# The first two modulation vectors of layer 0 from slabs of columns, and two of the other four as dots on VectorE

## The chip, the cores and the metric

The kernel runs on one NeuronCore of a Trainium2 chip. The metric is the device time of one launch in microseconds. The core has a matrix engine (TensorE, PE in the profile, with PEld for its weight loads), VectorE (DVE), ScalarE (ACT) and GpSimd (POOL), each with its own queue of instructions that it takes in order, and a sync engine (SP) that issues nearly all loads from memory, also in order. An instruction that has to wait for a semaphore holds up everything behind it in its queue.

## The reference

Two layers work on 512 tokens `x` and on 256 context tokens `ctx`, both 1024 wide. Each layer draws six vectors from a condition, `c` for the tokens and `c_ctx` for the context: shift, scale and gate for the mixer (vectors 0, 1, 2), and shift, scale and gate for the FFN (3, 4, 5).

```python
mod  = silu(c)     @ ada_w[l] + ada_b[l]          # 1024 x 6144, six vectors of 1024
modc = silu(c_ctx) @ ada_w[l] + ada_b[l]
sh1, sc1, g1, sh2, sc2, g2 = split(mod, 6)
a  = rmsnorm(h,  norm1_g[l]) * (1 + sc1)  + sh1   # ac from hc with the context's vectors
...
u, v, q, k, vv = split(a @ w_in, ...)             # layer 0: v gated MLP, differential attention
q, k = rope(q), rope(k)                           # layer 1: sliding window attention with a sink
...
h = h + g1 * y
h = h + g2 * swiglu(rmsnorm(h, norm2_g[l]) * (1 + sc2) + sh2)
```

In layer 0 the keys and values of the context stand behind those of the tokens. The mixer needs vectors 0 and 1 of layer 0 before its first product; vectors 2 to 5 are wanted only after its attention.

## The kernel before

Everything is kept transposed: the 1024 features lie on the partitions as 8 tiles (`KT`), tokens along the free axis, 512 columns for `x` (`TX`) and 256 for the context (`TC`). Every large product runs as three fp32r matmuls, high by high, high by low and low by high parts (`mm3`, L96 to L102). A weight block comes through `unit` (L67): SP loads the raw block, ScalarE casts the high part (L75), and GpSimd subtracts to get the low part (L78). The rings behind it have 5 raw buffers and 6 finished ones, and layer 0's q/k weights have three buffers more (`wq`).

The code is written in the order in which the work is meant to go, and a scheduler that simulates a timeline turns it into one queue for each engine; `issue_after` holds an instruction behind another, and a buffer that is allotted again brings a wait for its last reader.

The stage that the change touches is the first part of `even()`, up to the gated products:

- *Start.* `x` is loaded in four pieces, then `ident`. ScalarE takes Silu of `c` and `c_ctx` into `cst`, a tile with 32 columns for each k of which two are not zero. `squares` (L185) and `rstd_diag` (L139, sums on TensorE at L150) give the norm of the tokens, and `spread` (L177) puts it on all partitions.
- *Vectors 1 and 0.* `ada_load` (L339) loads 1 MB pieces of 256 rows by 1024 columns into a ring of four buffers, `ar`. `ada_step` (L347) multiplies one 128-row part by `cst`: four matmuls with 32 rows of output each (L351); in fp32 each stands twice in the profile. `ada_out` (L354) copies the sum, transposes it and adds the bias, and so writes columns of `mod`. First all of vector 1 (scale) is summed, then L394 multiplies the eight tiles of `x` by scale and norm, then all of vector 0 (shift). Between the steps stand filler matmuls without a use of their own (`warm`, L373; L376 issues them).
- *q and k in two halves* (L441). Each half makes four outputs of 128 rows from 8 tiles; for tile k it loads one 256 KB q/k block. In half 0 the shift is added on the way (L457 on ScalarE for the high part, L458 on VectorE for the low part). The context is loaded after the slabs, its norm formed inside half 0, and its eight tiles modulated by `modulate` (L190): VectorE multiplies (L193), ScalarE adds the shift and rounds (L194), VectorE subtracts for the low part (L195). After the token products of a half come those with the context, and `rope` (L242): a shuffle and a product on VectorE (L245, L246), a product and a sum on GpSimd (L247, L248).
- *Vectors 2 to 5* are done as 16 more steps (2 and 3 together, then 4 and 5), strewn through the halves and the following v products (L492) by `ada_ahead`, which loads, and `ada_some`, which computes. These steps have 1 MB each and the same four buffers.
- *v products*, then the attention of the first heads and the gated products (accumulated in `pf`).

Layer 1 has another way to form such vectors, which the changed kernel uses too. `ada_c` (L204) loads `c` spread over all partitions and takes its Silu; `ada_dot` (L219) multiplies a tile of transposed weights by it on VectorE and adds along the row (L222):

```python
self.nc.vector.scalar_tensor_tensor(junk, t, 1.0, self.cb[who], ALU.mult, ALU.mult,
                                    accum_out=self.acc[who][:, col:col + 1])
```

`ada_fin` (L225) adds the bias. One such dot gives 128 values of one vector for one of the two conditions.

Of the kernel before, what the change touches and what calls it, by code (L numbers as in the profile page):

```python
# [14 lines left out]
P = 128  # L15
# [11 lines left out]
class Builder:  # L27
# [286 lines left out]
    def even(self):  # L314
        tc, nc, a = self.tc, self.nc, self.a
        self.open_ring(512, 5, 6)
        self.adap = tc.alloc_tile_pool(name="ada0", bufs=1, side="left", reuse_waits="tile")
        self.ropep = tc.alloc_tile_pool(name="rope0", bufs=1, side="left", reuse_waits="tile")
# [13 lines left out]
        self.ident = self.load(p0, a["ident"], [P, P], "ident")  # L332
# [6 lines left out]
        def ada_load(j, n, k):  # L339

            m = 2 // n
            t = self.adap.tile([P, m, n * D], F32, name=self.uid("ar"), tag="ar", bufs=4)
            src = a["ada0"][k * P:(k + m) * P, j * D:(j + n) * D].rearrange("(k p) c -> p k c", p=P)
            self.last_slab = nc.sync.dma_start(t, src)
            return [t[:, i, :] for i in range(m)]
# [8 lines left out]
        def ada_out(j, n, ps, pt):  # L354
# [8 lines left out]
            for who in range(2):  # L363
                nc.vector.tensor_tensor(q(self.mod[who]), v[:, :, :, who], q(self.adab), ALU.add)
                for i in range(j, j + n):
                    if i in (1, 4):
                        m = self.mod[who][:, i * KT:(i + 1) * KT]
                        nc.vector.scalar_tensor_tensor(m, m, 1.0, self.gain(i // 3, 0), ALU.add, ALU.mult)
            return row
# [9 lines left out]
        slabs = sum([ada_load(1, 1, k) for k in range(0, KT, 2)], [])  # L379
        self.adab = self.load(p0, a["ada_b"], [P, 96], "adab")  # L380
        self.gains = self.load(p0, a["gains"], [P, 5 * KT], "gains")
        rd = self.rstd_diag([(sq, TX)], 1.0 / D)[0]
        ps0 = self.fill()
        for k in range(KT):
            ada_step(ps0, k, slabs[k])
            if k % 2:
                slabs += ada_load(0, 1, k - 1)
            if k == 3:
                rx = self.spread(rd)
            warm(slabs[k][:, :P], 2)  # L390
        scaled = self.bank()
        ada_out(1, 1, ps0, scaled)
        for k in range(KT):
            nc.vector.scalar_tensor_tensor(hx[k], hx[k], self.modcol(0, 1, k, 0), rx, ALU.mult, ALU.mult)  # L394
        ps0 = self.fill()
        for k in range(KT):
# [17 lines left out]
        def ada_some():  # L414
            if loaded:
                j, k, t = loaded.pop(0)
                if k == 0:
                    ps_of[j] = self.fill()
# [985 lines left out]
```

## Time and profile before

| | |
|---|---|
| time, median of 3 runs | 1640.96 us (1637.72 to 1641.31) |
| profiled execution, from its first to its last instruction | 1641.9 us, mean granted clock 0.977 |
| TensorE busy | 1542.8 us (94%) |
| VectorE, ScalarE, GpSimd busy | 1073.0 (65%), 724.5 (44%), 766.9 us (47%) |
| moved by DMA | 161.98 MB, mean 99 GB/s |
| chain of waits | 69% on TensorE |

The profile is of one further execution; for it only the span from its first to its last instruction is known, and the runs give whole device times. A row of the trace gives the time from the start of the span, the duration, the engine, the line, the operation, the buffer written and the buffers read, and in brackets the idle time before it and what ended it. A group row gives a count and the busy time. The table of stretches has, for each engine, the busy time and the number of instructions, and behind that the granted clock of TensorE, the share of the 16 DMA engines that was busy, and the rate.

### The profile page before, as it was taken

Reading aid. Unit: us, or ns where it says so; the run is one execution under the profiler, and the core shown is the slowest. Engines: PE = TensorE matmul, PEld = TensorE weight load, DVE = VectorE, ACT = ScalarE, POOL = GpSimd, SP = SyncE. Lnnn points to the kernel's source line nnn. Section 1 sums busy time; section 2 is a strip of 40 time slices with the busy share of each in tenths; the row PEclk is TensorE's granted clock in tenths of the full one; section 3 lists DMA queues with packets and bytes.
Section 4 is the critical chain, followed back from the end, with each engine's and each line's share of the span. In section 5 each row is a group of like instructions: output and inputs, shape, how many; then the busy total and the mean of one; then the engine's idle time right before and its main releaser. Section 6 shows DMA issues by size and latency. Waiting matters only on the chain.

```text
span 1641.9 us, 24642 instructions
## 1 busy us (share of the span) xinstructions
PE 1542.8 (94%) x9547; PEld 1367.1 (83%) x9547; DVE 1073.0 (65%) x1980; ACT 724.5 (44%) x1472; POOL 766.9 (47%) x543
## 2 busy tenths in 40 slices
PE   6999989999999999999999988999989999999996
PEld 4776877899899889998989978777868989898886
DVE  4621788756857788666665585665667857666665
ACT  2423675645533233333333244555664544444443
POOL 0463221062157666666666316532222466675662
PEclk9999989999999999999999999999999999999998
DMA  8744100141223343343432012110233222322201
GB/s 317 298 153 169 40 7 1 65 139 68 76 79 116 105 139 131 105 150 126 142 131 77 27 51 91 52 33 25 74 116 123 65 103 92 101 90 103 90 27 52
DMA packets 47957, 161.98 MB, mean 99 GB/s; under 512 B 5472, under 2 KB 9952, under 8 KB 40160
## 3 DMA queue, kind: packets, MB, share of 16 engines
q1 hardware_dynamic: 47696, 160.28, 28.4%
q8 instruction: 75, 1.23, 0.3%
q14 instruction: 42, 0.34, 0.1%
q10 hardware_dynamic: 144, 0.13, 0.0%
HBM read 158.29 MB, written 2.10 MB: 98 GB/s over the span
## 4 chain that ended last, share of the span: by engine, by line
PE 69%; DVE 11%; POOL 6%; DMA 5%; ACT 4%; issue 3%; POOLq 0%; SPq 0%; DVEq 0%; ACTq 0%
PE pw L100 9%; PE pw L101 9%; PE pw L102 9%; PE pb L100 7%; PE pb L101 7%; PE pb L102 7%; POOL w L917 5%; DMA raw<-ffn_in 3%; PE pf L100 3%; PE pf L101 2%; PE pf L102 2%; PE pb L1257 2%; PE pb L1246 2%; PE pf L351 2%; DVE t L968 2%
## 5 line engine op out<-in xcount | busy, mean ns | idle before, releaser
L100 PE MATMUL pw<-ax,w 128*128 128x384 f32 (+2 forms) x732 | 237.5, 328 | 16.1 <-DVE q L1012 6.7
L101 PE MATMUL pw<-ax,w 128*128 128x384 f32 (+2 forms) x732 | 237.9, 325 | 4.1 <-DVE ax L458 2.5
L78 POOL TENSOR_TENSOR w<-raw,w 128x512 fp32r<-128x512 f32 (+1 forms) x84 | 127.6, 1526 | 243.2 <-ACT w L75 220.8
L102 PE MATMUL pw<-ax,w 128*128 128x384 f32 (+2 forms) x732 | 236.7, 325 | 2.1 <-POOL w L917 2.1
L917 POOL TENSOR_TENSOR w<-raw,w 128x512 fp32r<-128x512 f32 x119 | 177.7, 1507 | 54.2 <-ACT w L913 53.4
L917 POOL TENSOR_TENSOR w<-t,w 128x512 fp32r<-128x512 f32 x90 | 133.4, 1482 | 139.9 <-ACT w L913 136.5
L100 PE MATMUL pb<-hh,w 128*128 128x512 f32 x480 | 167.3, 362 | 12.8 <-ACT hh L116 8.3
L766 DVE SCALAR_TENSOR_TENSOR xT<-pb,mod,xT 128x512 f32<-128x512 f32 (+3 forms) x208 | 144.5, 704 | 43.8 <-PE pb L102 43.1
L101 PE MATMUL pb<-hh,w 128*128 128x512 f32 x480 | 171.2, 358 | 0.5 <-POOL hh L117 0.5
L102 PE MATMUL pb<-hh,w 128*128 128x512 f32 x480 | 170.7, 357 | 0.0
L100 PEld LDWEIGHTS pw<-ax,w 128*128 128x128 f32 x732 | 142.0, 195 | 27.2 <-DVE q L1012 8.1
L100 PE MATMUL pw<-T,w 128*128 128x384 f32 (+1 forms) x508 | 159.1, 314 | 4.8 <-DVE hs L1008 2.4
L101 PE MATMUL pw<-T,w 128*128 128x384 f32 (+1 forms) x508 | 158.6, 312 | 4.0 <-DVE T L117 4.0
L102 PE MATMUL pw<-T,w 128*128 128x384 f32 (+1 forms) x508 | 158.2, 312 | 0.0
L101 PEld LDWEIGHTS pw<-ax,w 128*128 128x128 f32 x732 | 142.6, 195 | 12.1 <-DVE ax L458 3.4
L102 PEld LDWEIGHTS pw<-ax,w 128*128 128x128 f32 x732 | 142.4, 195 | 6.0 <-POOL w L917 2.7
L913 ACT CAST w<-t 128x512 fp32r<-128x512 f32 x104 | 64.5, 621 | 176.8 <-DVE t L968 122.5
L917 POOL TENSOR_TENSOR w<-rawo,w 128x512 fp32r<-128x512 f32 x63 | 94.1, 1493 | 66.5 <-ACT w L913 66.5
L100 PEld LDWEIGHTS pb<-hh,w 128*128 128x128 f32 x480 | 89.5, 189 | 27.0 <-ACT hh L116 10.8
L100 PEld LDWEIGHTS pw<-T,w 128*128 128x128 f32 x508 | 97.2, 192 | 9.7 <-DVE hs L1008 3.9
L101 PEld LDWEIGHTS pw<-T,w 128*128 128x128 f32 x508 | 97.4, 192 | 6.6 <-DVE T L117 4.6
L102 PEld LDWEIGHTS pb<-hh,w 128*128 128x128 f32 x480 | 90.3, 188 | 13.1
(363 smaller groups left out, 4056.7 us busy)
## 6 DMA issues: line engine op xcount, KB each, us to landing
raw<-ffn_in SPq DMA_DIRECT2D x44, 1024.0 KB, 4.9
ar<-ada SPq DMA_DIRECT2D x24, 1024.0 KB, 7.3
ar<-ada SPq DMA_DIRECT2D x48, 512.0 KB, 3.5
rawo<-ffn_out SPq DMA_DIRECT2D x44, 512.0 KB, 3.9
raw<-odd_out SPq DMA_DIRECT2D x32, 256.0 KB, 2.7
raw<-qk SPq DMA_DIRECT2D x16, 256.0 KB, 7.9
raw<-uv SPq DMA_DIRECT2D x16, 256.0 KB, 2.7
raw<-even_out SPq DMA_DIRECT2D x8, 512.0 KB, 4.2
```

The costliest lines, as they stand in the source:

```text
L78: eng.tensor_tensor(lo, raw, hi.bitcast(F32), ALU.subtract)
L100: mm(out, s[0], m[0], start=start, stop=False, **kw)
L101: mm(out, s[0], m[1], start=False, stop=False, **kw)
L102: return mm(out, s[1], m[0], start=False, stop=stop, **kw)
L351: nc.tensor.matmul(ps[32 * q:32 * q + 32, :w], cst[:, k, :], t[:, w * q:w * q + w], start=k == 0, stop=k == KT - 1, skip_group_check=True)
L766: self.nc.vector.scalar_tensor_tensor(h, ps[:, r], self.modcol(l, j, m, who), h, ALU.mult, ALU.add)
L913: nc.scalar.copy(t[:, 0, :], src)
L917: eng.tensor_tensor(t[:, 1, :], src, t[:, 0, :].bitcast(F32), ALU.subtract)
L968: nc.vector.tensor_tensor(t, x, y, how)
L1246: last = nc.tensor.transpose(pt[:, x * P:(x + 1) * P], es[2 * (x % 2) + x // 2][:, kb * P:(kb + 1) * P], self.ident)
L1257: nc.tensor.matmul(po[64 * h:64 * h + 64, :], V[vb][:, 64 * g:64 * g + 64], t[:, h * TC:h * TC + TC], start=kb == 0, stop=kb == nb - 1, sk ...
```

## The change

The weights of vectors 0 and 1 are laid out anew on the host: slab k holds, in 1 MB without gaps, the columns of both vectors that tile k needs, for all eight row tiles (`ada_s`). So tile k of `x` can be modulated when slab k alone has been projected. `first_rows` multiplies a slab by `cst`, four row tiles side by side in the four quarters of the partitions, and `first_cols` adds the four partial sums and transposes them in one step, with two small matmuls by `sel`; the results go into `first`. The tiles of `x` are multiplied by the norm first, then scaled and shifted by one VectorE instruction, then split. The products of tile k - 2 follow the projection of slab k. The fillers are now six behind each of the first three slabs, and those behind vectors 1 and 0 go.

Vectors 2 and 3 are transposed on the host (`ada_t`) and done as dots on VectorE: eight tiles of 1 MB, four dots each, strewn through the same places by `ada_some`. Vectors 4 and 5 stay steps on TensorE, and come behind them. The ring `ar` has three buffers in place of four, and the pool also holds the two spread conditions (`cb`). `ident`, the bias and the gains go to ScalarE's queue for loads; the context is loaded behind slab 3, and the spread conditions and the rope tables behind the last q/k block of half 0. The context is modulated between the products of tiles 6 and 7 and reads `first`. Line numbers in the diff's `first_rows` and after are those of the changed kernel: `slab` is L351, `first_rows` L355 to L364, `first_cols` L366 to L375, the product with the norm L486, scale and shift L493.

```diff
-        self.ident = self.load(p0, a["ident"], [P, P], "ident")
+        self.ident = self.load(p0, a["ident"], [P, P], "ident", eng=nc.scalar)
+        self.adab = self.load(p0, a["ada_b"], [P, 96], "adab", eng=nc.scalar)
+        self.gains = self.load(p0, a["gains"], [P, 5 * KT], "gains", eng=nc.scalar)
 
...
-        def ada_load(j, n, k):
-
-            m = 2 // n
-            t = self.adap.tile([P, m, n * D], F32, name=self.uid("ar"), tag="ar", bufs=4)
-            src = a["ada0"][k * P:(k + m) * P, j * D:(j + n) * D].rearrange("(k p) c -> p k c", p=P)
-            self.last_slab = nc.sync.dma_start(t, src)
-            return [t[:, i, :] for i in range(m)]
+
+        sel = self.adap.tile([P, 2], F32, name="sel")
+        nc.vector.tensor_reduce(sel, self.ident.rearrange("p (q c) -> p c q", q=4)[:, 0:2, :], axis=AX, op=ALU.add)
+        one_b = self.adap.tile([P, KT], F32, name="one_b")
+        nc.vector.tensor_scalar(one_b, self.adab[:, KT:2 * KT], 1.0, None, ALU.add)
+        first = self.adap.tile([P, 2, KT, 2], F32, name="first")
+
+        def slab(k):
+            t = self.adap.tile([P, 2 * D], F32, name=self.uid("ar"), tag="ar", bufs=3)
+            self.last_slab = nc.sync.dma_start(t, a["ada_s"][k])
+            return t
+
+        def first_rows(t):
+
+            ps = self.fill()
+            for r in range(2):
+                for q in range(4):
+                    k = 4 * r + q
+                    nc.tensor.matmul(ps[32 * q:32 * q + 32, :2 * P], cst[:, k, :], t[:, 2 * P * k:2 * P * k + 2 * P],
+                                     start=r == 0, stop=r == 1, skip_group_check=True)
+            row = self.adap.tile([P, 2 * P], F32, name=self.uid("row"), tag="row", bufs=2)
+            nc.scalar.copy(row, ps[:, :2 * P])
+            return row
+
+        def first_cols(k, row):
+
+            pt = self.bank()
+            for n in range(2):
+                nc.tensor.matmul(pt[:, 2 * n:2 * n + 2], row[:, n * P:(n + 1) * P], sel, start=True, stop=True,
+                                 skip_group_check=True)
+            nc.vector.tensor_scalar(first[:, 0, k, :], pt[:, 0:2], one_b[:, k:k + 1], self.gain(0, 0)[:, k:k + 1],
+                                    ALU.add, ALU.mult)
+            nc.vector.tensor_scalar(first[:, 1, k, :], pt[:, 2:4], self.adab[:, k:k + 1], None, ALU.add)
+
+        def ada_load(j, k):
+
+            t = self.adap.tile([P, 2 * D], F32, name=self.uid("ar"), tag="ar", bufs=3)
+            if j < 4:
+                r = ((j - 2) * KT + 2 * k) * P
+                t = t.rearrange("p (k c) -> p k c", k=2)
+                nc.sync.dma_start(t, a["ada_t"][r:r + 2 * P, :].rearrange("(k p) c -> p k c", p=P))
+            else:
+                nc.sync.dma_start(t, a["ada0"][k * P:(k + 1) * P, :])
+            return t
 
...
                 nc.vector.tensor_tensor(q(self.mod[who]), v[:, :, :, who], q(self.adab), ALU.add)
-                for i in range(j, j + n):
-                    if i in (1, 4):
-                        m = self.mod[who][:, i * KT:(i + 1) * KT]
-                        nc.vector.scalar_tensor_tensor(m, m, 1.0, self.gain(i // 3, 0), ALU.add, ALU.mult)
-            return row
+                m = self.mod[who][:, 4 * KT:5 * KT]
+                nc.vector.scalar_tensor_tensor(m, m, 1.0, self.gain(1, 0), ALU.add, ALU.mult)
...
         sq = self.squares(hx, TX)
-        slabs = sum([ada_load(1, 1, k) for k in range(0, KT, 2)], [])
-        self.adab = self.load(p0, a["ada_b"], [P, 96], "adab")
-        self.gains = self.load(p0, a["gains"], [P, 5 * KT], "gains")
         rd = self.rstd_diag([(sq, TX)], 1.0 / D)[0]
-        ps0 = self.fill()
-        for k in range(KT):
-            ada_step(ps0, k, slabs[k])
-            if k % 2:
-                slabs += ada_load(0, 1, k - 1)
-            if k == 3:
-                rx = self.spread(rd)
-            warm(slabs[k][:, :P], 2)
-        scaled = self.bank()
-        ada_out(1, 1, ps0, scaled)
-        for k in range(KT):
-            nc.vector.scalar_tensor_tensor(hx[k], hx[k], self.modcol(0, 1, k, 0), rx, ALU.mult, ALU.mult)
-        ps0 = self.fill()
-        for k in range(KT):
-            ada_step(ps0, k, slabs[KT + k])
-            warm(slabs[KT + k][:, :P], 3)
-        row = ada_out(0, 1, ps0, scaled)
-        warm(row[:, :P], 6)
-
 
         qk = {}
         AX_ = [self.ax() for _ in range(KT)]
         axx, axc = [[[t[:, c] for t in A] for A in AX_] for c in (slice(0, TX), slice(TX, TA))]
-        rest = [(j, k) for j in (2, 4) for k in range(KT)]
+        rest = [(j, k) for j in (2, 3) for k in range(KT // 2)] + [(4, k) for k in range(KT)]
...
             for _ in range(min(n, len(rest))):
                 j, k = rest.pop(0)
-                loaded.append((j, k, ada_load(j, 2, k)[0]))
+                loaded.append((j, k, ada_load(j, k)))
         def ada_some():
             if loaded:
                 j, k, t = loaded.pop(0)
+                if j < 4:
+                    for n in range(2):
+                        for who in range(2):
+                            self.ada_dot(0, j, 2 * k + n, t[:, n, :], who)
+                    if k == KT // 2 - 1:
+                        for who in range(2):
+                            self.ada_fin(0, j, who)
+                    return
                 if k == 0:
                     ps_of[j] = self.fill()
...
-        with tc.issue_after(self.last_slab.ins):
-            ctx_load()
+        def products(k):
+            for n in range(4):
+                self.mm3(accx[n], W[k][n], axx[k], k == 0, k == KT - 1)
+
         for half, heads in enumerate(((0, 1), (2, 3))):
-            w2 = [self.wide(), self.wide()]
-            accx = [w[:, h * 512:(h + 1) * 512] for w in w2 for h in range(2)]
-            W = []
+            W, rows = [], {}
+            if half:
+                w2 = [self.wide(), self.wide()]
+                accx = [w[:, h * 512:(h + 1) * 512] for w in w2 for h in range(2)]
             for k in range(KT):
                 t = self.adap.tile([P, 2, 512], F32R, name=self.uid("wq"), tag="wq", bufs=3) if k % 3 == 2 else None
+                if half == 0:
+                    s = slab(k)
+                    rows[k] = first_rows(s)
+                    if k < 3:
+                        warm(s[:, :P], 6)
                 with tc.issue_after(self.last_slab.ins) if half == 0 else ExitStack():
                     W.append(self.blocks(a["qk"][half, k], 512, t=t))
-                    if half == 0:
-                        if k > 4:
-                            with tc.issue_after(self.last_w.ins):
-                                ada_ahead(1)
-                        if k == 7:
-                            tabs += [self.load(self.ropep, a[n], [P, TX], n) for n in ("cos", "sin")]
+                    if half == 0 and k == 3:
+                        ctx_load()
                 if half == 0:
-                    t, sh = hx[k], self.modcol(0, 0, k, 0)
-                    nc.scalar.activation(axx[k][0], t, AF.Identity, bias=sh)
-                    nc.vector.scalar_tensor_tensor(axx[k][1], t, sh, axx[k][0].bitcast(F32), ALU.add, ALU.subtract)
-                elif k % 2:
+                    if k == 0:
+                        rx = self.spread(rd)
+                    for i in range(2 * k, 2 * k + 2) if k < 4 else ():
+                        nc.vector.tensor_tensor(hx[i], hx[i], rx, ALU.mult)
+                    if k == 2:
+                        w2 = [self.wide(), self.wide()]
+                        accx = [w[:, h * 512:(h + 1) * 512] for w in w2 for h in range(2)]
+                    if k > 1:
+                        products(k - 2)
+                    first_cols(k, rows.pop(k))
+                    nc.vector.tensor_scalar(hx[k], hx[k], first[:, 0, k, 0:1], first[:, 1, k, 0:1], ALU.mult, ALU.add)
+                    self.split(*axx[k], hx[k])
+                    if k == 6:
+                        rd = self.rstd_diag([(self.squares(hc, TC), TC)], 1.0 / D)[0]
+                    continue
+                if k % 2:
                     ada_ahead(1)
                     ada_some()
-                for n in range(4):
-                    self.mm3(accx[n], W[k][n], axx[k], k == 0, k == KT - 1)
-                if half == 0 and k == 4:
-                    rd = self.rstd_diag([(self.squares(hc, TC), TC)], 1.0 / D)[0]
-                if half == 0 and k == 5:
-                    rc = self.spread(rd)
-                    for i in range(KT):
-                        self.modulate(hc[i], TC, self.modcol(0, 1, i, 1), self.modcol(0, 0, i, 1), rc, axc[i])
+                products(k)
+            if half == 0:
+                with tc.issue_after(self.last_w.ins):
+                    for who in range(2):
+                        self.ada_c(who)
+                    tabs += [self.load(self.ropep, a[n], [P, TX], n) for n in ("cos", "sin")]
+                    ada_ahead(2)
+                products(KT - 2)
+                rc = self.spread(rd)
+                for i in range(KT):
+                    self.modulate(hc[i], TC, first[:, 0, i, 1:2], first[:, 1, i, 1:2], rc, axc[i])
+                products(KT - 1)
             for n in range(4):
                 evacuate(accx[n], n, slice(0, TX), heads)
...
-    r["ada0"] = c(A["ada_w"][0])
+    w = A["ada_w"][0]
+    ss = np.stack([w[:, D:2 * D], w[:, :D]], 1).reshape(KT, P, 2, KT, P)
+    r["ada_s"] = c(ss.transpose(3, 1, 0, 2, 4).reshape(KT, P, 2 * D))
+    r["ada_t"] = c(w[:, 2 * D:4 * D].T)
+    r["ada0"] = c(w[:, 4 * D:])
```

1 line of the change is left out of this document (added).

## The prediction

> **What bounds the kernel now.** I read the page's busy times and chain first, then the stretches of the first 165 us, then the rows of the places that the change touches.
>
> ```profile
> span 1641.9 us, 24642 instructions
> PE 1542.8 (94%) x9547; PEld 1367.1 (83%) x9547; DVE 1073.0 (65%) x1980; ACT 724.5 (44%) x1472; POOL 766.9 (47%) x543
> PE 69%; DVE 11%; POOL 6%; DMA 5%; ACT 4%; issue 3%; POOLq 0%; SPq 0%; DVEq 0%; ACTq 0%
> core 0: us, PE busy (x) PEld busy (x) DVE busy (x) ACT busy (x) POOL busy (x), PEclk, DMA share, GB/s
> 11.90:39.89 27.99, 27.54 (x234) 17.13 (x234) 10.93 (x35) 3.99 (x11) 0.59 (x1) 1.00 0.93 339
> 39.89:65.20 25.31, 22.51 (x108) 15.11 (x110) 17.14 (x30) 9.56 (x19) 11.62 (x9) 1.00 0.73 277
> 65.20:96.00 30.80, 30.80 (x189) 25.53 (x182) 15.30 (x29) 11.99 (x24) 21.73 (x16) 1.00 0.64 227
> 96.00:164.72 68.72, 68.72 (x382) 49.01 (x381) 13.77 (x24) 19.86 (x32) 28.55 (x22) 1.00 0.46 166
> 39.89 0.73 PE L100 MATMUL pw<-ax,w 128*128 128x512 f32 x2 [0.42 <-ACT ax L457]
> 164.72 0.39 PE L100 MATMUL pf<-ax,w 128*128 128x512 f32 x1
> ```
>
> TensorE is the bound. Its first 28 us are only modulation steps and fillers, at 339 GB/s of loads. The q/k products start at 39.89 and the gated branch (pf) at 164.72: this stage of 124.8 us is what the change rebuilds. From 65.20 on TensorE never idles in it. VectorE is busy 13.77 of the last 68.72 us, but GpSimd 28.55. Everything behind 164.72 keeps its order up to small swaps, so what this point moves, the end moves.
>
> **Prices.**
>
> ```profile
> GB/s 94 395 405 410 336 382 333 384 374 143 188 410 422 374 325 19 236 377 413 289 11 69 135 235 84 262 45 221 2 305 283 290 409 369 311 70 25 45 66 66
> raw<-ffn_in SPq DMA_DIRECT2D x44, 1024.0 KB, 4.9
> SPq L344 <- PE pw L376: 10.9, 3, 6.1
> 9.27 0.63 ACT L185 ACTIVATE t<-hx 128x512 f32<-128x512 f32 x1 [0.30 <-DMA hx<-xT]
> 11.93 2.05 PE L150 MATMUL pb<-ones,sq 128*128 128x128 f32 x8 [11.93 <-DVE sq L187]
> 13.91 1.08 PE L351 MATMUL pf<-ar,cst 128*32 128x256 f32 x8
> 17.95 0.64 PE L351 MATMUL pf<-ar,cst 128*32 128x256 f32 x8
> 37.97 1.50 PE L376 MATMUL pw<-t,ones 128*128 128x128 f32 x12
> 20.28 1.02 PE L177 MATMUL pb<-q,ones 128*128 128x512 f32 x2
> 128.48 1.00 PE pf L351 x8
> 133.78 1.00 PE pf L351 x8
> L222 DVE SCALAR_TENSOR_TENSOR junk<-ar,cb x64: 1206/1220/2626, 499.3 to 892.8; 128x1024 bf16<-128x1024 f32 x64
> 62.64 0.87 DVE L193 SCALAR_TENSOR_TENSOR t<-hc,mod,pb 128x256 f32<-128x256 f32 x2 [7.70 <-PE pb L177]
> 63.70 0.89 DVE L195 SCALAR_TENSOR_TENSOR ax<-t,mod,ax 128x256 fp32r<-128x256 f32 x2 [0.18 <-ACT ax L194]
> 78.31 0.74 DVE L245 STREAM_SHUFFLE sh<-f 128x512 f32<-128x512 f32 x1
> 79.08 0.69 DVE L246 TENSOR_TENSOR f<-f,cos 128x512 f32<-128x512 f32 x1
> 64.65 1.28 POOL L78 TENSOR_TENSOR wq<-raw,wq 128x512 fp32r<-128x512 f32 x1 [11.04 <-ACT wq L75]
> L207 ACT ACTIVATE cb<-cb x2: 1045/1054/1062, 354.4 to 355.4; 128x1024 f32<-128x1024 f32 x2
> 26.88 5.35 DVE L394 SCALAR_TENSOR_TENSOR hx<-hx,mod,pb 128x512 f32<-128x512 f32 x8
> 595.54 1.22 DVE L222 SCALAR_TENSOR_TENSOR junk<-ar,cb 128x1024 bf16<-128x1024 f32 x1
> 595.77 2.15 POOL L917 TENSOR_TENSOR w<-sq,w 128x512 fp32r<-128x512 f32 x1 [1.61 <-ACT w L913]
> 596.69 0.08 DVE L222 DVE_READ_ACCUMULATOR junk<-ar,cb 128x1 f32 x1
> 596.81 2.19 DVE L222 SCALAR_TENSOR_TENSOR junk<-ar,cb 128x1024 bf16<-128x1024 f32 x1
> 449.36 0.44 PE L100 MATMUL pw<-ax,w 128*128 128x384 f32 x1 [0.75 <-ACT w L913]
> 452.09 0.69 PE L102 MATMUL pw<-ax,w 128*128 128x384 f32 x1 [2.11 <-POOL w L917]
> 457.38 0.52 PE L100 MATMUL pw<-T,w 128*128 128x384 f32 x1
> 457.98 0.33 PE L102 MATMUL pw<-T,w 128*128 128x384 f32 x1
> ```
>
> The first line is the load rate in slices of 4 us from 0: about 400 GB/s when nothing holds it, 2.6 us per MB. A 1 MB load lands 4.9 us after its issue. Products of 512 columns come every 0.23 us (from one L351 row at 128.48 to the next at 133.78 lie 18 of them and one step: 5.3 us, so a step costs 1.2 with its change-over), those of 256 columns every 0.12. A dot costs 1.22 + 0.08 = 1.3 us.
>
> The four rows from 595.54 carry most of this forecast. GpSimd's 1.3 us subtraction begins under a running dot and takes 2.15, to 597.92; the next dot begins under it and takes 2.19, to 599.00. Neither advances while the other runs, and whoever waits goes next: with both queues full, one dot passes per GpSimd instruction, some 1.1 us each. Instructions with one SBUF operand and one PSUM operand (L193) are not held.
>
> **The change, part by part.**
>
> *The head.* The scale slabs and then the shift slabs, 8.4 MB in all before the first product, become eight slabs of 1 MB (L351), each followed by its 256 KB of qk; tile k needs slab k alone. x is in at 9.27 as now, so slabs 0, 1, 2 land near 12.0, 15.3, 18.5. Slab 3 takes slab 0's buffer (three instead of four). Slab 0 is read by 8 slow matmuls from 13.98 (11.93 + 2.05; twice the 1.08 row) and six fillers (1.50 warm, about twice that here); it is free near 18.7, and slab 3 lands at 24 (1 to 2 us of idle queue). ident, adab and gains move past SP to ACT's queue and are in long before use: nothing. The spread of rx (1.02) stands behind slab 1's fillers; VectorE scales by it from 22.3 (8 x 0.67 = 5.4, from L394), writes the columns of tiles 0 to 2, and tile 0 is ready near 29: first product 29.6 against 39.89, **-10.3**. The eight tiny column pairs cost 0.05 each on PE.
>
> *Half 0 after that.* VectorE and ACT work through tiles 0 to 3 in order, and TensorE waits: 26.5 to 29.6, two products, then to 32.2. The rows from 452.09 show what that does: after 0.75 and 2.11 us of idle time close together products ran 0.32 instead of 0.17 us apart for 5.6 us. I take that once, 2.9 us. Slab 7 then waits for slab 4's buffer (near 41), as three slabs do now (the SPq line, 10.9 us), and lands at 46. On ACT the row copies of tiles 4 and 5 stand behind the casts of qk 6 and 7, tile 5's split behind the two Silus of c (1.05 us each), tile 6's behind a cast of half 1: these hold tiles 5 to 7 by a few us. My walk ends the tiles' products at 36.8, 40.8, 43.8, 47.8, 52.0, 56.3, 59.3 and 65.2 (tile 7's low half is ready at 62.9, behind three dots). That is 7.6 us idle or slow, where now it is 3.7 (72 products by 61.8 instead of by 58): **+4**. Slabs 4 to 7 are projected inside the stage: **+4.8** with their columns.
>
> *The removed steps.* Vectors 2 and 3 leave TensorE: 8 steps x 1.2 and one set of transposes, **-10.1**. Their 32 dots cost TensorE nothing only while VectorE keeps up.
>
> *The dots in VectorE's queue.* In the built program the first dot stands before tile 7's columns and before the diagonal of the context's norm, and needs slab 8 (ar_543), which follows qk 7, both c broadcasts, cos, sin and four qk blocks: 56 us. Behind it the eight context tiles (L193, L195) alternate with 14 dots and four rope pairs. VectorE's own time from there to the last context tile is 28 us; GpSimd has 10 to 12 instructions ready beside it (rope and the low parts of half 1). Walked in the alternation of the rows above (a dot 1.1, L246 0.6, L195 0.3, GpSimd 1.15 each turn), the context tiles are split at 65.1 (two), 73.3, 76.8, 82.3, 84.0, 93.4 and 94.8, where 80 would be reached with none of it. TensorE, which takes the context tiles in between half 1's products, waits at tiles 2, 4 and 6: **+7.7**.
>
> *The v products.* Vector 4 and 5's steps stay on TensorE, but step 0 needs the buffer of the sixth dotted tile, step 1 the seventh's, step 3 the eighth's. My walk ends their dots at 118.9, 131.4 and 142.1 (own time 1.3 each, ropes of half 1 and the low parts of v between them). Each tile lands 5 us later; TensorE, first wanting step 0 at 118.8, waits 5, 2.5 and 3: **+10.5**. It takes its queue in order, so v products that are ready wait too. After step 3: 1.2 + 76 x 0.23 + four steps 4.8 + transposes 0.5, so pf begins near 171.
>
> Sum: -10.3 + 4 + 4.8 - 10.1 + 7.7 + 10.5 = **+6.6**; the walk itself gives 171 - 164.7 = +6. The context's larger loads (two 512 KB broadcasts) lie in queues counted above. The broadcasts' Silus are L207 rows of 1.05. Layer 1 and the FFN are untouched: nothing.
>
> For the alternation the bounds are none and full: 33 us of GpSimd instructions against 63 us of VectorE's own put the last dot between 119 (TensorE then sets the end at about 149, -15) and 152 (+16). I take 142, nearer the full end, since the 595 rows show strict turns, but not at it: GpSimd's rope steps themselves wait for VectorE. For the cold clock the bounds are 0 and two bouts (6 us).
>
> The Trainium skill, DMA: Bandwidth & Descriptors, Specifications, gives about 358 GB/s per core from HBM. This trace disagrees: several slices above show 395 to 422. By that figure slab 8 would land some 5 us later, and the sum, an estimate from that page, would be near +11.
>
> The Trainium skill, TensorE: Matmul & The Clock Gate, section "Why this matters for your kernels", says that an idle gap over about 3 us halves the clock. By it the two gaps of 3.1 and 2.1 us around one short burst could go either way; the sum would be +3.7 without the bout. The 452.09 row, where two smaller gaps sufficed, decides for it.
>
> **Rivals.**
> *VectorE keeps up.* One mechanism: turns on the port cost less than walked, because GpSimd's queue stalls on ropes and casts and leaves VectorE alone. For it: VectorE is busy only 13.77 of 68.72 us in the last stretch. Against: the dots alone add 42 us, and GpSimd is busy 28.55 there. It decides at a last dot before 136, where the end equals 164.7; a last dot at 124 gives -12, time 1629.
> *Even.* Earlier start and waits cancel within 3.3 us: 1641.
> *Loads late.* Slab 3, slab 7 and slab 8 each come later than reckoned because SP's queue stands behind a buffer's release; SP already waits 10.9 us in this way. Each us of slab 8 moves all dots by a us: three of them give +15, 1656.
> *The start does not move at all* (ACT's queue holds tile 0 until the context, at 27, is squared): then -10.3 is lost, 1657. Against: tile 0's split needs only four of the eight squares before it.
>
> **Numbers.** The profiled span, 1641.9, is just above the runs (1637.72 to 1641.31, median 1640.96), so I add +6 to the median: 1647. Chances: forecast (+2 to +11) 0.48, VectorE keeps up 0.27, even 0.13, loads late 0.10, start unmoved 0.02. About 0.2%, 3.3 us, is what a measurement of this kernel can tell from no change. Slower: 0.43 of the forecast lies beyond 3.3 us, and both late cases, 0.55; same: 0.13 and the forecast's other 0.05, 0.18; faster 0.27. The range runs from 1628 to 1659; for the forecast alone 1643 to 1652.
>
> **What would show it.** First product near 30; TensorE at half pace once between 32 and 38; slab 7 issued near 41; VectorE over 9 tenths busy from 56 to past 135, with dots of 1.2 and of 2.2 us; TensorE waiting on the context's L195 and then on the first, second and fourth step's loads; pf near 171. I am wrong if the last dot ends before 136, or if VectorE idles for slabs.

## The result, and the profile after

The changed kernel took 1651.13 us in the median of four runs (1650.12 to 1659.99), the kernel before 1639.47 us beside it: a ratio of 1.0077 (95% interval 1.0049 to 1.0105), slower by some 12 us. The forecast was 1647 us, slower, within 1628 to 1659.

The page of the changed kernel (span, busy times, chain):

```profile
span 1648.3 us, 24560 instructions
PE 1529.5 (93%) x9451; PEld 1363.3 (83%) x9451; DVE 1124.8 (68%) x2066; ACT 727.8 (44%) x1479; POOL 782.8 (47%) x543
PE 56%; DVE 11%; POOL 6%; DMA 5%; ACT 4%; issue 3%; POOLq 0%; ACTq 0%; DVEq 0%; SPq 0%
```

TensorE is busy 13.3 us less than before, VectorE 51.8 us more, and the span is 6.4 us longer: TensorE did less and waited more. The same stretches as in the prediction:

```profile
11.90:39.89 27.99, 24.55 (x170) 17.02 (x171) 17.08 (x48) 10.96 (x24) 9.77 (x7) 0.94 0.83 317
39.89:65.20 25.31, 22.75 (x141) 16.76 (x140) 15.24 (x42) 7.89 (x15) 2.67 (x3) 1.00 0.82 307
65.20:96.00 30.80, 26.51 (x155) 23.45 (x154) 30.73 (x47) 10.47 (x23) 22.88 (x14) 0.94 0.35 112
96.00:164.72 68.72, 62.61 (x327) 45.69 (x326) 44.20 (x57) 13.60 (x26) 38.93 (x22) 0.95 0.65 230
```

VectorE is full from 65.20 to 96.00 (30.73 of 30.80 us, before 15.30), TensorE has gaps where it had none, and the granted clock, 1.00 in all stretches before, is 0.94 and 0.95 in three of these. What TensorE waits for from 60 to 170 us (line, releaser, total, times, longest), and where, with the marks at which the stage begins and ends:

```profile
PE pf L391 <- DMA ar<-ada: 6.1, 3, 3.0
PE pb L100 <- ACT ax L194: 3.9, 2, 3.3
PE pw L100 <- ACT ax L116: 1.9, 1, 1.9
PE pb L101 <- DVE ax L195: 1.0, 1, 1.0
```

```profile
28.28 0.73 PE L100 MATMUL pw<-ax,w 128*128 128x512 f32 x2 [0.81 <-ACT ax L116]
30.57 0.79 PE L101 MATMUL pw<-ax,w 128*128 128x512 f32 x1 [1.55 <-DVE ax L117]
61.32 0.74 PE L100 MATMUL pw<-ax,w 128*128 128x512 f32 x2 [1.87 <-ACT ax L116]
87.85 0.50 PE L100 MATMUL pb<-ax,w 128*128 128x256 f32 x2 [3.26 <-ACT ax L194]
121.23 1.07 PE L391 MATMUL pf<-ar,cst 128*32 128x512 f32 x8 [3.02 <-DMA ar<-ada]
122.96 0.63 PE L102 MATMUL pw<-w,ax 128*128 128x512 f32 x1
123.38 0.63 PE L100 MATMUL pw<-w,ax 128*128 128x512 f32 x1
135.34 1.09 PE L391 MATMUL pf<-ar,cst 128*32 128x512 f32 x8 [2.37 <-DMA ar<-ada]
169.06 0.40 PE L100 MATMUL pf<-ax,w 128*128 128x512 f32 x1
338.23 1.16 PE L697 MATMUL pf<-sguT,f 128*128 128x128 f32 x8
```

The first product comes at 28.28 instead of 39.89. Then TensorE waits for tile 7 behind dots (61.32), for a context tile (87.85) and for the loads of steps (121.23, 135.34), and behind the long waits the products come 0.43 us apart for a while (122.96 to 123.38) instead of 0.23. The gated products begin at 169.06, where it was 164.72: of 11.6 us, all is lost and 4.3 more.

The last row is a second mark, the mixing of the gated part behind the attention heads; before, it stood here:

```profile
330.86 1.16 PE L654 MATMUL pf<-sguT,f 128*128 128x128 f32 x8
```

There the distance is 7.4 us: 3.0 more were lost in the attention heads. From this mark to the end, where no edit changes the work, the traces of all kernels take 1303.6 to 1314.2 us without order, so the experiments are read at the two marks, and the times decide between kernels. A trace is one execution: those of "steps first", "GpSimd idle", "one vector as dots" and "changed, again" are of the slowest of their runs, that of the changed kernel is of its fastest.

### The profile page after: what moved, and what is told of

Its sections match the earlier page's. It is cut to its first block, busy times and chain, and to the rows that moved or that the text cites. A ratio compares the mean times of both kernels' runs of the same rounds, so it can differ in the third digit from the quotient of the medians.

```text
span 1648.3 us, 24560 instructions
## 1 busy us (share of the span) xinstructions
PE 1529.5 (93%) x9451; PEld 1363.3 (83%) x9451; DVE 1124.8 (68%) x2066; ACT 727.8 (44%) x1479; POOL 782.8 (47%) x543
## 4 chain that ended last, share of the span: by engine, by line
PE 56%; DVE 11%; POOL 6%; DMA 5%; ACT 4%; issue 3%; POOLq 0%; ACTq 0%; DVEq 0%; SPq 0%
PE pw L100 7%; PE pw L101 7%; PE pw L102 7%; PE pb L100 7%; PE pb L101 7%; PE pb L102 7%; POOL w L960 4%; DMA raw<-ffn_in 4%; PE pb L1300 2%; PE pb L1289 2%; PE pf L100 2%; PE pf L101 2%; PE pf L102 2%; DMA rawo<-ffn_out 1%; DVE t L1011 1%
## 5 line engine op out<-in xcount | busy, mean ns | idle before, releaser
L78 POOL TENSOR_TENSOR w<-raw,w 128x512 fp32r<-128x512 f32 (+1 forms) x84 | 131.4, 1571 | 232.9 <-ACT w L75 209.0
L222 DVE SCALAR_TENSOR_TENSOR junk<-ar,cb 128x1024 bf16<-128x1024 f32 x96 | 148.9, 1551 | 0.7
L100 PEld LDWEIGHTS pb<-hh,w 128*128 128x128 f32 x480 | 89.3, 188 | 26.1 <-ACT hh L116 10.0
L100 PEld LDWEIGHTS pw<-T,w 128*128 128x128 f32 x508 | 97.2, 192 | 10.7 <-DVE hs L1051 3.9
L75 ACT CAST w<-raw 128x512 fp32r<-128x512 f32 (+1 forms) x100 | 64.5, 652 | 92.3 <-PE pb L102 48.2
```

Source lines behind the costliest of these rows:

```text
L75: self.last_cast = nc.scalar.copy(hi, raw)
L78: eng.tensor_tensor(lo, raw, hi.bitcast(F32), ALU.subtract)
L100: mm(out, s[0], m[0], start=start, stop=False, **kw)
```

## The experiments

The theory was that dots and GpSimd's instructions take turns, and that the context's tiles and the steps of vectors 4 and 5 wait for the dots; the first rival, that the loss lies in the head, where slabs now stand inside half 0. All marks together, in us. The ratio is to the kernel before, which ran beside each group (with its 95% interval); between groups the ratios are compared, not the medians:

| kernel | gated products | mixing | median | ratio |
|---|---|---|---|---|
| before | 164.72 | 330.86 | 1639.47 to 1641.71 | 1 |
| changed | 169.06 | 338.23 | 1651.13 | 1.0077 (1.0049 to 1.0105) |
| changed, again | 170.97 | 342.46 | 1655.20 | 1.0075 (1.0055 to 1.0095) |
| slabs alone | 164.24 | 331.09 | 1644.71 | 1.0027 (1.0012 to 1.0042) |
| steps first | 155.66 | 342.98 | 1647.75 | 1.0042 (1.0024 to 1.0061) |
| dots behind the context | 168.89 | 343.88 | 1655.46 | 1.0093 (1.0075 to 1.0110) |
| GpSimd idle | 157.48 | 324.84 | 1631.65 | 0.9937 (0.9913 to 0.9961) |
| in turns | 157.01 | 337.47 | 1644.71 | 1.0029 (1.0017 to 1.0042) |
| slabs alone, four buffers | 162.04 | 329.03 | 1643.11 | 1.0010 (0.9993 to 1.0027) |
| dotted tiles early | 160.54 | 329.17 | 1638.64 | 0.9993 (0.9977 to 1.0008) |
| one vector as dots | 161.81 | 330.08 | 1640.36 | 0.9998 (0.9987 to 1.0010) |
| early, four buffers | 159.07 | 325.87 | 1635.76 | 0.9962 (0.9948 to 0.9976) |
| changed, four buffers | 164.32 | 331.84 | 1643.52 | 1.0013 (0.9996 to 1.0031) |

**Slabs alone.**

```diff
-        rest = [(j, k) for j in (2, 3) for k in range(KT // 2)] + [(4, k) for k in range(KT)]
+        rest = [(j, k) for j in (2, 4) for k in range(KT)]
...
-                    for who in range(2):
-                        self.ada_c(who)
```

> The slabs alone: vectors 2 to 5 are 16 steps of two vectors on TensorE again, nothing on VectorE, three buffers as in the changed kernel. Theory (the dots cost what the removed steps gave, by their turns with GpSimd): the last token product of half 0 comes near 63.0 instead of 65.6, since tile 7 no longer stands behind three dots; from there to the gated products 102.6 us as in the kernel before (62.1 to 164.7), so they begin near 165.6, against 169.1 in the changed kernel, and the time is some 3.5 us below the changed kernel's. No idle time of TensorE on the context and on loads of steps between 66 and 160. Rival (the loss lies in the head, with slabs inside half 0 and cold clock, and the dots cost little): eight more steps of 1.2 us come on top, the gated products begin near 178, and the time is 8 us above the changed kernel's.

```profile
164.24 0.39 PE L100 MATMUL pf<-ax,w 128*128 128x512 f32 x1
PE pb L101 <- DVE ax L195: 2.7, 2, 1.4
```

164.24 was near the theory's 165.6 and far from the rival's 178. No wait on the context was expected, but there were 3.3 us. (The comparison with 62.1 in that text was a misreading: in the kernel before, the products of tiles 6 and 7 lie behind the context's first tiles.) So the new head, worth 11.6 us at the first product, is worth 0.5 us at the gated products: the slabs inside the stage, a slow clock (0.84 from 30 to 40 us) and the waits on the context eat it. And the dots, with 8 steps fewer on TensorE, cost 4.8 us where they should have saved 10.

**Steps first, dots behind.**

```diff
-        rest = [(j, k) for j in (2, 3) for k in range(KT // 2)] + [(4, k) for k in range(KT)]
+        rest = [(4, k) for k in range(KT)] + [(j, k) for j in (2, 3) for k in range(KT // 2)]
```

> The changed kernel with the order of the vectors turned: the eight steps of vectors 4 and 5 first (halves 0 and 1), the 32 dots of vectors 2 and 3 behind them, mostly in the v products. Theory: the context's tiles are held by no dot and the steps by no dotted buffer; TensorE has 92.5 us of work behind the last token product of half 0 (102.6 less 8 steps and their transposes), which comes near 63, so the gated products begin at 155 to 158, and the time is 11 to 14 us below the changed kernel's. Dots still take 1.2 or 2.2 us, but nobody waits. Rival (the loads of the stage are what is late, in whatever order): TensorE waits some 6 us on the steps' loads in half 1, and the gated products begin at 163 or later.

```profile
155.66 0.39 PE L100 MATMUL pf<-ax,w 128*128 128x512 f32 x1
PE pw L577 <- DVE vlo L117: 13.3, 1, 13.3
```

The mark stood in the forecast interval: without dots ahead of them neither the context nor the steps wait. The time did not follow: 11 to 14 us below the changed kernel were expected, and the median is 3.4 below. The last dot now begins at 166.5, and the first attention head's q and k and the low parts of v stand behind it on VectorE; TensorE waits 13.3 us for them. The debt had only moved. Whether q and k wait for the memory of the dots' buffers or for VectorE's queue alone, no run told apart.

**Dots behind the context's tiles.**

```diff
+                    with tc.issue_after(self.last_mod.ins):
                         for n in range(2):
                             for who in range(2):
                                 self.ada_dot(0, j, 2 * k + n, t[:, n, :], who)
```

> The changed kernel, but no dot is issued before the low part of the last context tile. Theory: waits on the context (4.3 us and a bout of slow clock) and tile 7's (2.6) go, but 11 dots that ran before 80 us now come behind the rest, the last dot ends at 144 to 151 instead of 138.5, and the steps' loads with it: TensorE waits 12 us or more on the steps' loads in the v products, and the gated products begin at 174 to 184, later than in the changed kernel. Rival (only the order of VectorE's queue in the context's stretch costs, the steps' waits are not tied to the dots): the gated products begin near 161.

```profile
PE pf L391 <- DMA ar<-ada: 10.9, 3, 8.0
168.89 0.48 PE L100 MATMUL pf<-ax,w 128*128 128x512 f32 x1
```

The last dot ended at 144.8, as the theory had it, and the steps' waits grew from 6.1 to 10.9 us (12 or more was expected); the rival's 161 fell. But the mark did not move (174 to 184 was expected): TensorE waits 4.8 us more on the steps and 2.6 us on low parts of weights, which is new, but some 4.7 us less on the context and tile 7, and the slow clock costs some 1.8 us less. So these two terms of the forecast behave like one debt of VectorE, paid at one place or the other.

**GpSimd idle.**

```diff
+        if self.no_pool:
+            nc.scalar.copy(lo, raw)
+            return hi, lo
...
+        if self.no_pool:
+            nc.scalar.copy(sh, sh)
+            nc.scalar.copy(out, sh)
+            return
```

> The changed kernel with GpSimd idle from the first weight to the end of the v products: the low parts of these weights are copies of the raw weights made by ScalarE, and the two GpSimd steps of each rope are copies on ScalarE, so the products come out with wrong values and unchanged sizes. Theory (turns on the port): no dot takes over 1.3 us, the last one ends at 120 to 126 instead of 138.5, the context's low parts take 0.45 each, and the gated products begin at 156 to 160. Rival (VectorE's own time is too long, GpSimd does not matter): the last dot ends beyond 133, and the gated products begin at 166 or later.

The dots of the changed kernel and of this one (minimum, median and maximum in ns):

```profile
L222 DVE SCALAR_TENSOR_TENSOR junk<-ar,cb x32: 1206/1227/2315, 57.1 to 136.3; 128x1024 bf16<-128x1024 f32 x32
```

```profile
L225 DVE SCALAR_TENSOR_TENSOR junk<-ar,cb x32: 1194/1219/1228, 59.4 to 117.5; 128x1024 bf16<-128x1024 f32 x32
157.48 0.39 PE L103 MATMUL pf<-ax,w 128*128 128x512 f32 x1
```

This kernel leaves out the low parts of the weights and the second half of each rope, so it is a probe and no version to use. With nothing on GpSimd beside them no dot takes over 1.23 us (the mean of the 32 falls from 1.63 to 1.22), the last ends at 118.7, a little before the expected 120 to 126, and the steps' waits are gone. The time is 0.63% below the kernel before. The number and the order of the dots are the same, and the changed kernel had no wait of TensorE on GpSimd itself in this stage (the list of waits above). So it is GpSimd's work that lengthens the dots. In the changed kernel it looks like this (VectorE, then GpSimd):

```profile
71.47 1.24 DVE L311 TENSOR_TENSOR nlam<-sm 128x1 f32<-128x1 f32 x1
131.86 2.19 DVE L222 SCALAR_TENSOR_TENSOR junk<-ar,cb 128x1024 bf16<-128x1024 f32 x1
134.09 2.16 DVE L222 SCALAR_TENSOR_TENSOR junk<-ar,cb 128x1024 bf16<-128x1024 f32 x1
136.30 2.17 DVE L222 SCALAR_TENSOR_TENSOR junk<-ar,cb 128x1024 bf16<-128x1024 f32 x1
```

```profile
71.22 1.46 POOL L78 TENSOR_TENSOR w<-raw,w 128x512 fp32r<-128x512 f32 x1
132.93 2.24 POOL L78 TENSOR_TENSOR w<-raw,w 128x512 fp32r<-128x512 f32 x1
135.13 4.48 POOL L248 TENSOR_TENSOR f<-f,sh 128x512 f32<-128x512 f32 x2
```

Each dot begins inside a GpSimd instruction and ends some 1.1 us after it, and each GpSimd instruction does the same inside a dot: the one at 132.93 ends at 135.17, the dot begun at 134.09 at 136.25, the next one of GpSimd at 137.37. Even a VectorE instruction on one column (L311), which takes 0.15 us elsewhere, lasts 1.24 us, until the GpSimd instruction beside it has ended. The Trainium skill, SBUF — State Buffer, section "Who interferes with whom", says that a VectorE instruction with two SBUF inputs contends with a GpSimd instruction that reads SBUF; by these rows the trace agrees.

**Steps and dotted tiles in turns, then earlier, then one vector only.**

```diff
+        rest = [(dots if c == "D" else steps).pop(0) for c in "SSSDSDSDSDSDSDDD"]   # in turns
+        rest = [(dots if c == "D" else steps).pop(0) for c in "SSSDSDDSDDSDDDSS"]   # early
+        rest = [(dots if c == "D" else steps).pop(0) for c in "SSSSDSDSDSDSSSSS"]   # one vector
```

> The changed kernel with steps and dotted tiles in turns: three steps of vectors 4 and 5 first, then a dotted tile and a step alternately, three dotted tiles last. Theory: the first run of four dots comes when six of the eight context tiles are multiplied, so the context waits 3 us at most (as with slabs alone) and no step waits over 2 us; the dots are spread from about 75 to 155, the last ends before 158, and the six low parts of v behind them cost TensorE little (under 4 us, against 13.3 with the order turned). The gated products begin at 155 to 159 and the time is 1632 to 1637, below the kernel before. Rival (32 dots are too many for VectorE in this stage in any order, since the turns with GpSimd take what order gives): the last dot ends beyond 165, TensorE waits over 8 us on the low parts of v or on steps, and the time is 1641 or more.

> As the kernel with steps and dotted tiles in turns, but with the dotted tiles earlier: eight dotted tiles in places 4, 6, 7, 9, 10, 12, 13, 14 of 16 instead of 4, 6, 8, 10, 12, 14, 15, 16, and two steps last. Theory (the last dot sets when the buffers' memory is free for the first attention head's q and k, and VectorE's 11 us of work on these and on v's low parts stand behind it): the last dot ends at 148 to 153 instead of 160.5, TensorE waits 0 to 4 us instead of 11.0 on the low parts of v, the gated products begin at 156 to 159, and the mixing of the gated part begins near 329 to 333 instead of 337.5; time 1635 to 1640. Rival (the wait follows the number of dots, since VectorE has no room for 32): the last dot moves by under 3 us, the wait stays over 8 us, time 1643 or more.

> The slabs, with vector 2 alone as 16 dots (places 5, 7, 9, 11 of 16) and vector 3 back on TensorE as four tiles of two short steps, behind the steps of vectors 4 and 5. Theory (what counts is VectorE's own time and turns against the room it has in this stage): TensorE's work is 5 us less than with slabs alone (8 steps of 1.2 become 8 of 0.55), the dots end before 125, nothing waits for them, the gated products begin at 158 to 160.5 (slabs alone: 164.2), TensorE waits under 2 us on the low parts of v, the mixing of the gated part begins at 324.5 to 327.5, and the time is 1633 to 1638, below the kernel before. Rival (any dots in this stage cost what they save): the gated products begin at 163 or later, or a wait of over 4 us stands behind them; time 1641 or more.

The waits on the low parts of v in the first two:

```profile
PE pw L578 <- DVE vlo L117: 11.0, 1, 11.0
```

```profile
PE pw L578 <- DVE vlo L117: 2.8, 1, 2.8
```

In turns, the last dot ended at 160.5, 2.5 us later than hoped, and the 11.0 us behind it were far over the expected 4: the theory's time failed, and the rival's (1641 or more) held, though not its last dot beyond 165. With the same 32 dots earlier the last one ends at 153.4 and 8.2 of the 11.0 us are gone, so the number of dots is not the limit; the gated products began 1.5 us later than expected, with 2.2 us on a step's load. One vector as dots leaves no wait behind, but the gated products begin at 161.81 (158 to 160.5 expected), with 3.4 us on the context: neither text was met, and the time equals the kernel before (1633 to 1638 expected).

**Four buffers.**

```diff
-            t = self.adap.tile([P, 2 * D], F32, name=self.uid("ar"), tag="ar", bufs=3)
+            t = self.adap.tile([P, 2 * D], F32, name=self.uid("ar"), tag="ar", bufs=4)
...
-... tag="wq", bufs=3) if k % 3 == 2 else None      # not in "slabs alone"
+... tag="wq", bufs=2) if k % 3 == 2 else None
...
-            row = self.adap.tile([P, 2 * P], F32, name=self.uid("row"), tag="row", bufs=2)   # nor this
+            row = self.adap.tile([P, 2 * P], F32, name=self.uid("row"), tag="row", bufs=1)
```

> The slabs alone, with four buffers for them instead of three. Theory (slab 3 and slab 7 stand in the queue for the release of a buffer, and everything behind them in that queue with them): slab 3 is issued near 9 instead of 17.8, and slab 7 some 8 us earlier than 38.7, the context and its norm with them; the waits of TensorE on the context's low parts (3.3 us) shrink to under 1 us, the first product stays at 28 to 29 (it needs slab 0 and the norm), the gated products begin at 160 to 162 instead of 164.2, and the time is 2 to 4 us below that of the slabs alone. Rival (the loads are bound by their rate, not by buffers): slab 3 lands no more than 2 us earlier, the gated products begin at 163.5 or later, time unchanged within 2 us.

> The kernel with the early dotted tiles, and four buffers for slabs, steps and dotted tiles instead of three; to make room, the copied rows have one buffer instead of two, and the third set of q/k weights two instead of three. Theory (a fourth buffer frees the queue of loads in the head, and unties steps from the dots two tiles before): slab 3 is issued near 9, the context's first wait (2.6 us) goes, TensorE's wait of 2.2 us on a step's load goes, the gated products begin at 154 to 157 instead of 160.5, the last dot ends at 146 to 150, the wait on the low parts of v stays under 5 us, the mixing of the gated part begins at 322 to 326, and the time is 1631 to 1636, below both kernels. Rival (the dots are the limit, and the smaller weight buffers hold the products): the mixing begins at 328 or later, time 1638 or more.

> The changed kernel in its own order, with the same four buffers (and the same two smaller rings). Theory: a step's load no longer waits for the dots three tiles before it but four before, so it is issued one dotted tile (6 to 9 us) earlier; the 6.1 us of waits on steps' loads shrink to 2 or less, the waits on the context (4.3 us) stay, since the dots stand in the same places of VectorE's queue; the gated products begin at 162 to 166 instead of 169.1, and the time is 3 to 7 us below the changed kernel's. Rival (the last dots set the end through the memory of the attention's first q and k, whatever the steps do): the start of the mixing of the gated part moves by less than 2 us from 338.2.

Slab 3's issue with three buffers (changed kernel) and with four (early tiles), with the marks of the latter:

```profile
18.15 0.33 SPq L351 DMA_DIRECT2D ar<-ada_s  x1
```

```profile
8.33 0.33 SPq L351 DMA_DIRECT2D ar<-ada_s  x1
27.87 0.80 PE L370 MATMUL pb<-sel,row 128*128 128x2 f32 x4 [0.55 <-ACT row L363]
159.07 0.39 PE L100 MATMUL pf<-ax,w 128*128 128x512 f32 x1
325.87 1.16 PE L698 MATMUL pf<-sguT,f 128*128 128x128 f32 x8
```

Slab 3 goes out 9.8 us earlier. With slabs alone the waits on the context vanish and the mark moves by 2.2 us, to the edge of what was expected. Its median is 1.6 us lower, less than expected, and the intervals of the two ratios overlap: for the time this is not clear of noise. In the changed kernel's own order, with the two smaller rings as well, the gated products move by 4.7, the mixing by 6.4 and the median by 7.6 us (11.7 against the changed kernel of the same runs, below). One wait on a step's load remains, where 2 us were expected:

```profile
PE pf L391 <- DMA ar<-ada: 5.7, 1, 5.7
```

The ratio falls from 1.0077 to 1.0013. That the changed kernel went from four buffers to three was thus most of its loss; and with four, the kernels with slabs alone and with dots come out alike (1.0010 and 1.0013, within their intervals). With the dotted tiles early the fourth buffer gives a version that beats both kernels: 1635.76 us, 0.9962 (0.9948 to 0.9976). The gated products came 2 us later than expected there; the first product already stood at 29.61 instead of 28.28, behind waits on the copied rows (L370), which have one buffer there. The mixing was in its interval, and TensorE no longer waits for the low parts of v.

**The changed kernel again.**

> The changed kernel once more, beside the same runs of the kernel before. Every theory expects the marks of the stage to stand where they were, within 1 us: gated products at 169.1, mixing of the gated part at 338.2, and the time near 1651. If the time lies within 4 us of the kernel before, the surplus of some 5 us of the runs over the two traces (11.7 against 6.4) was chance in the stretches behind, which no edit touches.

```profile
PE pf L391 <- DMA ar<-ada: 8.0, 4, 2.8
342.46 1.16 PE L697 MATMUL pf<-sguT,f 128*128 128x128 f32 x8
```

The marks did not stand: the steps' waits were 8.0 instead of 6.1 us and the mixing came 4.2 us later than in the first trace. The time is again 0.75% over the kernel before, so the surplus of the runs was not chance behind the stage.

## Why the prediction was right, and where it was not

*The head* was right: 28.28 against 29.6, and slab 7 was issued at 39.18 against 41.

*Half 0* ended as walked: its last token product begins at 65.37 (forecast 65.2 for the end). One bout of slow clock was there; it cost 1.7 us instead of 2.9 (0.79 of the clock over 8 us, below).

*The removed steps* (-10.1) gave nearly what was reckoned: in "steps first" the gated products begin 8.6 us before those of slabs alone. Both have waits in it (2.7 and 3.3 us); without these it is 8.0 us, with more slow clock in "steps first" (0.72 against 0.84 from 30 to 40 us).

*The context's tiles* (+7.7): waits of 0.69, 3.26 and 1.03 us, and a bout of slow clock of 1.7 that was not in the sum, 6.7 in all. *The v products* (+10.5): 6.1 us of waits on loads (8.0 in the second trace) and two bouts, 9.5. The forecast had the waits too long and the clock's share too small; that together they nearly met is luck. The last dot ended at 138.5 against 142, between the bounds of 119 and 152. The lower bound's end of 149 was too low, though: with no turns at all TensorE reaches the gated products at 157.48.

*The gated products* were forecast at 171 and stood at 169.06 and 170.97: +4.3 and +6.2 against +6.

The step that failed is the one that carried this to the end: "Everything behind 164.72 keeps its order up to small swaps, so what this point moves, the end moves." The small swaps cost. From the gated products to the mixing lie 166.1 us before, 169.2 and 171.5 in the two traces of the changed kernel, and 167.5 with the fourth buffer. From 175 to 330 us TensorE waits for exponentials, first in the kernel before, then in the changed one:

```profile
PE pw L534 <- ACT e L538: 4.7, 4, 1.7
PE pw L535 <- ACT e L538: 2.5, 1, 2.5
```

```profile
PE pw L578 <- ACT e L581: 5.8, 3, 2.7
PE pw L577 <- ACT e L581: 5.3, 5, 2.5
```

That is 3.9 us more on scores that wait for exponentials, of the size of the distance; in the second trace it is 4.2 us more, and with the fourth buffer, where the distance grew by 1.4, 1.9 us more. Which swap in the queues makes it was not tried and stays open. The time came 4 us above the forecast. The kernel before was itself 1.5 us faster in these runs than the median that the forecast started from, so +11.7 stands against +6, and the interval of the ratio (+8 to +17 us) does not hold +6: the direction and the stage were right, the size at the end was not.

Of the rivals, *VectorE keeps up* named the right condition (a last dot before 136) and GpSimd's idle run met it; here it was 138.5. With the fourth buffer the last dot ended at 133.7 and the gated products began at 164.32, at the 164.7 that this rival gave for 136. *Loads late* was not a case of its own: loads of steps were late by the release of buffers that dots held, as in the forecast. Its +15 does not follow from its own rule, by which three us of slab 8 on top of +6 give +9. *The start does not move* fell with the first product at 28.28, *even* with the time.

## What to carry to other kernels

An engine that looks idle by its busy share can be full once its instructions take turns with another's: price an added operation at the alternation, and look for the pairs of engines that exclude each other. When work moves to such an engine, its debt is paid wherever the first consumer stands (context, steps, v), so moving the order moves the wait; earlier starts and one more buffer removed it. A kernel that gives up a buffer for room should be priced by who then waits for the release, on every queue behind it.

## What the runs showed of the hardware that was not expected

The granted clock fell more often than reckoned. Four stretches of the changed kernel, each with a wait of TensorE at its start or just ahead of it:

```profile
28.00:36.00 8.00, 6.17 (x26) 3.98 (x26) 7.57 (x16) 4.58 (x10) 2.49 (x2) 0.79 1.00 405
86.00:92.00 6.00, 4.15 (x14) 3.46 (x15) 6.00 (x8) 1.42 (x3) 4.61 (x4) 0.72 0.00 0
118.00:126.00 8.00, 4.98 (x19) 3.14 (x19) 7.96 (x11) 0.42 (x1) 8.00 (x5) 0.79 0.35 140
132.00:140.00 8.00, 5.63 (x25) 3.20 (x27) 7.64 (x8) 0.00 (x0) 8.00 (x5) 0.79 0.74 262
```

Each bout is worth 1.7 us (8 times 0.21, 6 times 0.28). Here idle times of 2.37, 3.02 and 3.26 us were each followed by one, and so was the group of 0.51, 0.81 and 1.55 us ahead of and among the first products. But it is no threshold: in the second trace of the same kernel two stretches behind idle times of 2.78 and 2.25 us stand so:

```profile
124.00:128.00 4.00, 4.00 (x20) 3.30 (x19) 4.00 (x6) 0.62 (x1) 4.00 (x3) 1.00 0.38 136
150.00:154.00 4.00, 3.73 (x13) 1.81 (x14) 0.00 (x0) 0.00 (x0) 0.00 (x0) 0.57 1.01 415
```

The longer one (at 121) left the clock at 1.00, the shorter one (at 150) did not. The Trainium skill, TensorE: Matmul & The Clock Gate, section "What's actually happening", gives a window of about 3.4 us that is free-running, so that the moment at which the clock changes depends on where in the window the first product lands. The products stay slow for 3 to 4 us (122.22 to 125.94 in the first trace), near that length, and chance plays a part; but the idle times that sufficed are all shorter than the window, and that its phase decides is not shown by any run here. In a sum for this kernel, a wait of 2 to 3 us on TensorE is better priced with some 1 to 1.7 us on top, an estimate from these bouts.
